# Layer 1's depthwise convolution spread over its projections and attention, branch products put between gate streams, two modulation sections moved into layer 0's attention

## The chip, the cores and the metric

One Trainium2 chip, one of its cores. The metric is the device time of one execution in microseconds (us). The kernel before took 1978.15 us (median of 3 runs, 1974.14 to 1978.68).

## What is computed

Two layers of a diffusion backbone over 512 latent tokens with 256 context tokens before them. Each layer has a token mixer with three branches (pooling, attention, convolution) under gates, then an MLP. Layer 1 is the last and computes latent outputs only; its context rows give keys and values alone. All arithmetic is float32.

```python
hl = _modulate(xl, sh1_l, sc1_l)                      # LayerNorm, then scale and shift from w_mod
ul_pool, ul_q, ul_k, ul_v, ul_conv, ul_gate = _split_in(hl @ w_in[i] + b_in[i])
ol = _latent_attention(ql, kl, vl, kc, vc, attn_sink[i])   # +-128 tokens, plus all context keys
y_conv = silu(layer_norm(depthwise_conv31(a * sigmoid(b)))) @ w_proj
yl = (g_pool * y_pool + g_attn * y_attn + g_conv * y_conv) @ w_out   # g = sigmoid(gates)
xl = _post_norm(xl, g1_l, yl, ln1_g[i], ln1_b[i])
xl = _post_norm(xl, g2_l, _mlp(_modulate(xl, sh2_l, sc2_l), ...), ln2_g[i], ln2_b[i])
```

`mod = silu(c) @ w_mod[i] + b_mod[i]` has six sections of 1024 (shift, scale, gate, for mixer and MLP); sections 3 and 4 are the MLP's shift and scale.

## The kernel before, in words

A float32 operand is kept as two fp32r halves (high and rest), so each product is three matmuls: high by high, rest by high, high by rest. Activations lie in `A` and `B` (tiles acta and actb, h and l; the names swap between layers), 8 slices of 128 channels by 768 columns. A weight unit is 128x512: one DMA into `raw`, a cast on ScalarE (`wh`, L134), a subtraction on GpSimd or VectorE (`wl`, L137). `weight_a` makes two units, one 128-column output tile for 8 contraction slices; `mm_a_steps` (L149) runs its 24 matmuls on 512 or 256 columns.

`w_phase` (L560) is the mixer of a layer. Its order: V and K projections, the queries of the first key-value head, the second pool tile; then the convolution (`conv`, L312): 31 chained VectorE instructions for each of two channel tiles; `cover` gives TensorE gate tiles meanwhile, for 145000 columns in layer 0 and 118000 in layer 1. Then pool products, LayerNorm of the convolution (`conv_norm`, a Sigmoid in it), and attention: 2 heads by 4 blocks (layer 0 has 4 more blocks for context). The queries of the second head are projected when its first block begins.

TensorE's order is written by hand: `tick` counts columns; `later` puts a step in a heap that falls due after so many columns, and between steps the generator `gated_steps` (L624) fills in. It runs 8 gate tiles for attention (to DRAM, `sgd`), then for each m a pool gate with its branch product (`branch_steps`, two contraction slices, 6 matmuls) and a conv gate with its product, and sends the sum to DRAM (`mfd`). A gate is a Tanh on ScalarE out of PSUM (L611); a product is combined with it on VectorE (L621). Gate and projection tiles take their PSUM banks from `psg` (two), branch products, the attention output and other small things from `psa` (two), scores and transposed probabilities from `pss` (two tiles of two banks). The other engines' instructions are ordered by a scheduler that keeps the program's priorities.

`pace` calls a generator once per so many columns. `mod_steps` (L173) makes one section: per contraction slice a chunk of `wmod`, and four matmuls of 32 weight columns by 256, one for each quarter of the PSUM partitions (float32, two TensorE records each). In layer 0, section 2 is paced over the projections; sections 3 and 4 over the closing stretch, which is the rest of the gates and then, for each m, the attention branch's product with `g` and `d` read back from DRAM (L827 to L835).

Of the kernel before, what the change touches and what calls it, by code (L numbers as in the profile page):

```python
# [18 lines left out]
P = 128  # L19
D = 1024  # L20
# [47 lines left out]
W_VAL = 9000  # L68
W_CONV0 = 145000
W_CONV1 = 118000  # L70
# [7 lines left out]
def backbone(ctx: ExitStack, tc: tile.TileContext, I: dict, out: bass.AP):  # L78
# [233 lines left out]
    def conv(pool, psum, cvec, gls, st):  # L312

        n = TL if st == 0 else TC
        ps = psum.tile([P, 1024], F32, tag="S", name=uid("cp"))
        accs = []
        for j in range(2):
            gl, run = gls[j, st], ps[:, j * 512:j * 512 + n]
            acc = pool.tile([P, n], F32, tag=f"ca{st}", name=uid("ca"), bufs=2)
            V.tensor_scalar(out=run, in0=gl[:, 0:n], scalar1=cvec[:, j, 0:1], scalar2=cvec[:, j, 31:32],  # L320
                            op0=ALU.mult, op1=ALU.add)
            for k in range(1, CK):
                V.scalar_tensor_tensor(out=run if k < CK - 1 else acc, in0=gl[:, k:k + n],
                                       scalar=cvec[:, j, k:k + 1], in1=run, op0=ALU.mult, op1=ALU.add)
            accs.append(acc)
        return accs

    def conv_norm(pool, scratch, cvec, accs, st, dst):
# [4 lines left out]
        for b0 in range(0, n, 256):  # L333
            pt, pb = bank(), bank()
# [12 lines left out]
            yield W_CN  # L347
            for j in range(2):
# [62 lines left out]
    def softmax_pv(pp, pss, g, Pt, vtiles, negm, sums, V_, sink, dst, qsl):  # L411
# [42 lines left out]
        t1 = pp.tile([64, 4, P], F32, tag="t1", name=uid("t1"), bufs=1)  # L454
        S.copy(t1, po[64:128, :].rearrange("p (a q) -> p a q", a=4))
        ot = pp.tile([P, 2, P], F32, tag="ot", name=uid("ot"), bufs=2)
# [6 lines left out]
    def attn_ctx(pp, pss, g, nb, Q, KH, KL, V_, nsink, sink, dst):  # L463
# [3 lines left out]
        for a in range(4):  # L467
            o = s[:, a * 256:(a + 1) * 256]
            T.matmul(o, Q[a][:, qsl], KH[g][:, CS], start=True, stop=False)
            T.matmul(o, Q[a][:, qsl], KL[g][:, CS], start=False, stop=True)  # L470
# [15 lines left out]
    def attn_lat(pp, pss, g, n, Q, KH, KL, V_, nsink, sink, dst, masks):  # L486
# [10 lines left out]
        for a in range(4):  # L497
            s = pss.tile([P, 1024], F32, tag="S", name=uid("S"))
            q = Q[a][:, qsl]
# [60 lines left out]
    def w_phase(i, A, B, has_ctx, pre, todo):  # L560
# [5 lines left out]
        with ExitStack() as ph:  # L566
# [8 lines left out]
            mg = ph.enter_context(tc.tile_pool(name=f"mg{i}", bufs=4 if todo else 6, reuse_waits="tile"))  # L575
            sgd = [dram.tile([P, W], F32, tag=f"sg{i}{m}", name=uid("sgd")) for m in range(KD)]
            mfd = [dram.tile([P, W], F32, tag=f"mf{i}{m}", name=uid("mfd")) for m in range(KD)]
            mix = ph.enter_context(ExitStack())
# [14 lines left out]
            if todo:  # L593
                pace((x for s in todo for x in mod_steps(i, s, 0, D, lambda: mg.tile(
                    [P, W], F32, tag="sg", name=uid("wm"))[:, :512])), 10000, 20000)
# [7 lines left out]
            def gate_steps(m, b):  # L603
# [10 lines left out]
            def branch_steps(w, ks, w0, g, outs, pool):  # L614

                while ks[0] not in mixed:
                    yield None
                for _, sl in outs:
                    ps = bank(pool)[:, :sl.stop - sl.start]
                    yield from mm_a_steps(w, B, ks, [(ps, sl)], w0)  # L620
                    V.scalar_tensor_tensor(out=g[:, sl], in0=g[:, sl], scalar=1.0, in1=ps,  # L621
                                           op0=ALU.add, op1=ALU.mult)

            def gated_steps():  # L624
                for m in range(KD):
                    g = yield from gate_steps(m, 1)
                    nc.sync.dma_start(out=sgd[m], in_=g)

                w, d, e, ahead = {}, {}, {}, 0 if todo else 2
                for m in range(ahead):  # L630
                    d[m] = yield from gate_steps(m, 0)
                for m in range(KD + 1):
                    if m + ahead < KD:
                        d[m + ahead] = yield from gate_steps(m + ahead, 0)
                    if m < KD:
                        w[m] = weight_a(I["wbr"][i, m][:, 0:4 * P])
                        yield from branch_steps(w[m], (0, 1), 0, d[m], outs_all, side["bank"])
                    if m:
                        e = yield from gate_steps(m - 1, 2)
                        yield from branch_steps(w.pop(m - 1), (2, 3), 2, e, outs_all, side["bank"])  # L640
                        G.tensor_tensor(out=d[m - 1], in0=d[m - 1], in1=e, op=ALU.add)
                        nc.sync.dma_start(out=mfd[m - 1], in_=d.pop(m - 1))

            mixed, side = set(), {"bank": psa}
# [11 lines left out]
            masks = kv.tile([P, 2, P], F32R, tag="masks", name=uid("masks"))  # L656
            KH = [kv.tile([P, TA], F32R, tag=f"kh{g}", name=uid("kh")) for g in range(NKV)]
            KL = [kv.tile([P, TA], F32R, tag=f"kl{g}", name=uid("kl")) for g in range(NKV)]
            V_ = kv.tile([P, 6, NKV, P], F32R, tag="V", name=uid("V"))

            def evac(ps, t):
                qf = kv.tile([P, TA], F32, tag="qf", name=uid("qf"))
                for st, p_ in enumerate(ps):
                    sl = (LS, CS)[st]
                    S.activation(qf[:, sl], p_, AF.Identity, bias=b_in[:, t:t + 1])
                return qf

            def query(Q, g, jj, temp):
                t = T_Q + 2 * g + jj
                qf = evac(proj(t, LC), t)  # L670
                rope(temp, qf, cs)
                for par in range(2):
# [16 lines left out]
            flush()  # L689

            vf = evac(proj(T_V, [LS, CS]), T_V)
# [14 lines left out]
            kf = evac(proj(T_K, [LS, CS]), T_K)  # L706
            rope(scratch("rt")[:, :TL], kf, cs)
            for g in range(NKV):
                r = slice(64 * g, 64 * g + 64)
                V.tensor_copy(KH[g][r, :], kf[r, :])  # L710
                S.copy(KH[g][64 - 64 * g:128 - 64 * g, :], kf[r, :])
                for r2 in (0, 64):
                    V.tensor_tensor(out=KL[g][r2:r2 + 64, :], in0=kf[r, :],
                                    in1=KH[g][r, :].bitcast(F32), op=ALU.subtract)
            Q = [kv.tile([P, W], F32R, tag=f"q{a}", name=uid("q")) for a in range(4)]
# [6 lines left out]
            def pool_products():  # L722
                for j in range(2):
# [6 lines left out]
                    for st, sl in outs_all:  # L730
                        n = TL if st == 0 else TC
                        ps = bank()[:, :n]
# [9 lines left out]
            accs = {st: conv(cp, pss, cvec, gls, st) for st, _ in outs_all}  # L742
            cover((W_CONV0 if has_ctx else W_CONV1) - W_PC)
            for wait in pool_products():
                cover(wait)
            mixed.add(0)
            cover(W_PC)
            flush()
            for st, _ in outs_all:
                for wait in conv_norm(cp, scratch, cvec, accs[st], st, B):  # L750
                    cover(wait)
            mixed.add(2)
            t12.close()
            pp = mix.enter_context(tc.tile_pool(name=f"pp{i}", bufs=1, side="right", reuse_waits="tile"))

            def items():
                for g in range(NKV):
                    if g:
                        Q[:] = [kv.tile([P, W], F32R, tag=f"q{a}", name=uid("q")) for a in range(4)]
                        for jj in range(2):  # L760
                            query(Q, g, jj, pp.tile([P, TL], F32, tag="rt", name=uid("rt"), bufs=1))
                    for n in range(4):
                        yield attn_lat(pp, pss, g, n, Q, KH, KL, V_, nsink, sink, B, masks)
# [49 lines left out]
            mixed.add(4)  # L813
            mix.close()
            if todo:
                for _ in pe["pace"]:
                    pass
            pace(None, 0)
# [3 lines left out]
            side["bank"] = psg  # L822
            if todo:
                pace((x for s in (3, 4) for x in mod_steps(i, s, 0, D, lambda: fin.tile(
                    [P, D], F32, tag="wm", name=uid("wm"), bufs=4))), 9000)
            drain(other)
            for m in range(KD):  # L827
# [4 lines left out]
                nc.sync.dma_start(out=d, in_=mfd[m])  # L832
# [3 lines left out]
            if todo:  # L836
                for _ in pe["pace"]:
# [231 lines left out]
    with tc.manual_schedule(engines={mybir.EngineType.PE}):  # L1069
# [69 lines left out]
        for i in range(DEPTH):  # L1139
            last = i == DEPTH - 1  # L1140
            w_phase(i, A, B, not last, pre, () if i else (2,))
# [87 lines left out]
```

## Time and profile before

| what | us |
|---|---|
| median of three runs | 1978.15 |
| the profiled execution, its own time | 1975.67 |
| its span, first to last instruction | 1973.9 |
| TensorE busy in the span | 1848.6 (94%) |
| VectorE / ScalarE / GpSimd busy | 1200.3 / 730.8 / 771.6 |
| mean granted TensorE clock, share of full | 0.978 |
| layer 0: attention | 244 to 476 |
| layer 0: closing stretch of the mixer | 476 to 543.2 |
| layer 1: projections and convolution | 1232 to 1353 |
| layer 1: attention | 1353 to 1528 |
| layer 1: closing stretch | 1528 to 1550.2 |

The times inside the span count from its first instruction. TensorE's records overlap: a matmul of 512 columns is shown with 0.39 us, and the next one begins 0.23 us later, so the work on this engine is counted by the distance between starts.

### The profile page before, as it was taken

The numbers are of one execution on the slowest core, as the hardware profiler recorded it, in microseconds if no ns is written. First come the engines' busy times: TensorE is split into PE (matmuls) and PEld (weight loads), VectorE is DVE, ScalarE is ACT, GpSimd is POOL, SyncE is SP. The second block draws the span as 40 slices with busy tenths as digits, with TensorE's granted clock in tenths as the row PEclk, the third lists the DMA queues.
The fourth block names the chain that finished last, engine by engine and source line by source line (L and its number), as shares of the span: only waits on it lengthen the run. The fifth ranks groups of instructions, "written<-read, shape, count | busy, mean of one in ns | idle before, by whom it ended". The sixth has DMA issues, their size and how long they took to land. (4 is left out here: it accounts for less than half of the span.)

```text
span 1973.9 us, 27007 instructions
## 1 busy us (share of the span) xinstructions
PE 1848.6 (94%) x9910; PEld 1548.4 (78%) x9910; DVE 1200.3 (61%) x2067; ACT 730.8 (37%) x1359; POOL 771.6 (39%) x629
## 2 busy tenths in 40 slices
PE   6999899899899999999999988999988989999997
PEld 4788788787678888888788868777866768888886
DVE  6489655654478946865533584786575784333356
ACT  4432255353234422233133344434444354333331
POOL 3653432322434422222122546664342554333343
PEclk8999999999999999999999989999999989999999
DMA  8523111114865434464422423141212753332341
GB/s 304 176 90 118 62 59 46 53 44 154 281 219 190 161 112 133 155 213 143 146 62 86 129 96 105 61 149 63 69 65 96 260 189 118 96 96 86 107 129 43
DMA packets 117557, 244.94 MB, mean 124 GB/s; under 512 B 14608, under 2 KB 16944, under 8 KB 117424
## 3 DMA queue, kind: packets, MB, share of 16 engines
q1 hardware_dynamic: 117424, 243.21, 38.0%
q8 instruction: 78, 1.28, 0.3%
q14 instruction: 55, 0.45, 0.1%
HBM read 223.20 MB, written 19.96 MB: 123 GB/s over the span
## 5 line engine op out<-in xcount | busy, mean ns | idle before, releaser
L137 POOL TENSOR_TENSOR wl<-raw,wh 128x512 fp32r<-128x512 f32 x371 | 516.7, 1405 | 783.6 <-ACT wh L134 698.9
L134 ACT CAST wh<-raw 128x512 fp32r<-128x512 f32 x506 | 310.8, 621 | 596.0 <-PE ps L167 292.1
L156 PE MATMUL ps<-actbh,wh 128*128 128x512 f32 (+1 forms) x1016 | 353.4, 348 | 14.3 <-DVE sg L621 6.9
L156 PE MATMUL ps<-actbl,wh 128*128 128x512 f32 (+1 forms) x1016 | 348.3, 343 | 3.1 <-POOL actbl L251 3.1
L156 PE MATMUL ps<-actbh,wl 128*128 128x512 f32 (+1 forms) x1016 | 347.8, 342 | 2.7 <-DVE rs L261 1.3
L156 PE MATMUL ps<-actah,wh 128*128 128x512 f32 (+1 forms) x928 | 331.4, 357 | 13.7 <-ACT actah L248 4.7
L156 PE MATMUL ps<-actal,wh 128*128 128x512 f32 (+1 forms) x928 | 327.4, 353 | 3.3 <-DVE actal L1097 1.9
L156 PE MATMUL ps<-actah,wl 128*128 128x512 f32 (+1 forms) x928 | 326.9, 352 | 0.4 <-POOL wl L137 0.3
L156 PEld LDWEIGHTS ps<-actbh,wh 128*128 128x128 f32 x1016 | 194.5, 191 | 45.2 <-DVE sg L621 10.0
L156 PEld LDWEIGHTS ps<-actbh,wl 128*128 128x128 f32 x1016 | 194.4, 191 | 25.6 <-DVE wl L137 2.4
L156 PEld LDWEIGHTS ps<-actbl,wh 128*128 128x128 f32 x1016 | 194.6, 192 | 23.3 <-POOL actbl L251 3.8
L156 PEld LDWEIGHTS ps<-actah,wh 128*128 128x128 f32 x928 | 177.5, 191 | 43.8 <-ACT actah L248 5.1
L156 PEld LDWEIGHTS ps<-actal,wh 128*128 128x128 f32 x928 | 177.6, 191 | 25.6 <-DVE actal L1097 2.2
L156 PEld LDWEIGHTS ps<-actah,wl 128*128 128x128 f32 x928 | 177.4, 191 | 24.2 <-POOL wl L137 1.0
L165 PE MATMUL ps<-wh,actah 128*128 128x512 f32 x480 | 192.6, 401 | 2.2 <-DVE acc L977 2.0
L167 PE MATMUL ps<-wh,actal 128*128 128x512 f32 x480 | 190.5, 397 | 3.5 <-DVE actal L251 3.5
L166 PE MATMUL ps<-wl,actah 128*128 128x512 f32 x480 | 190.1, 396 | 0.0
L137 DVE TENSOR_TENSOR wl<-raw,wh 128x512 fp32r<-128x512 f32 x135 | 127.8, 947 | 99.9 <-ACT wh L134 97.3
L204 DVE SCALAR_TENSOR_TENSOR wm<-wm,sc,wm 128x512 f32<-128x512 f32 x140 | 124.4, 924 | 67.1 <-DMA wm<-in_wmod 67.0
L970 DVE TENSOR_TENSOR acc<-ps,acc 128x512 f32<-128x512 f32 x140 | 94.7, 684 | 95.3 <-PE ps L167 95.2
L165 PE MATMUL ps<-wh,actbh 128*128 128x512 f32 (+1 forms) x328 | 127.2, 388 | 1.5 <-DVE fg L621 1.5
L166 PE MATMUL ps<-wl,actbh 128*128 128x512 f32 (+1 forms) x328 | 126.8, 387 | 1.0 <-POOL wl L137 1.0
(207 smaller groups left out, 2721.7 us busy)
## 6 DMA issues: line engine op xcount, KB each, us to landing
raw<-in_w SPq DMA_DIRECT2D x264, 256.0 KB
raw<-in_win SPq DMA_DIRECT2D x154, 256.0 KB
wm<-in_wmod SPq DMA_DIRECT2D x72, 512.0 KB
raw<-in_wout SPq DMA_DIRECT2D x56, 256.0 KB
wm<-in_wmod SPq DMA_DIRECT2D x48, 256.0 KB
raw<-in_wbr SPq DMA_DIRECT2D x32, 256.0 KB
x1d<-R SPq DMA_DIRECT2D x10, 512.0 KB
acc<-in_b SPq DMA_DIRECT2D x10, 512.0 KB
```

The source lines that it names most:

```text
L134: S.copy(wh, r)
L137: e.tensor_tensor(out=wl, in0=r, in1=wh[:].bitcast(F32), op=ALU.subtract)
L156: T.matmul(ps, w(hl, w0 + n), x[xi][:, k, sl], start=(start and first and hl == 0 and xi == 0), stop=(stop and last and hl == 1))
L165: T.matmul(ps, x[0][:, k0 + k, tsl], wh, start=(k == 0), stop=False)
L166: T.matmul(ps, x[0][:, k0 + k, tsl], wl, start=False, stop=False)
L167: T.matmul(ps, x[1][:, k0 + k, tsl], wh, start=False, stop=(k == n - 1))
L204: V.scalar_tensor_tensor(out=o, in0=x, scalar=sc[:, k, r:r + 1], in1=o, op0=ALU.mult, op1=ALU.add)
L970: V.tensor_add(a, ps, a)
```

## The change

1. Sections 3 and 4 of layer 0's modulation go from the closing stretch into attention, one step per 3500 columns; their chunks are 256 columns wide (three buffers), and `mod_steps` yields after each of the four matmuls where the chunk holds only one of them.
2. A branch product is no longer run behind its gate: `gate_steps` queues it in `pend` as one `piece` per stream, and a piece runs between the streams of the next gate, with its PSUM bank from `psg`.
3. In layer 1 the convolution is paced, one VectorE instruction per 2400 columns, from the V projection on, in two `psa` banks; pool products and `conv_norm` become steps that fall due; attention begins after 35000 columns of gates. The second head's queries are projected inside the first head's blocks. Pool parts go to DRAM and are read back when the conv part is there. V and the masks lie in free columns of `B`.
4. In both layers the high halves of K and Q are copied on ScalarE; the second copy of K's rest is a ScalarE copy too.

```diff
@@ mod_steps
                 T.matmul(ps[32 * j:32 * j + 32, :q], sc[:, k, :], w[:, o:o + q],
                          start=(k == 0), stop=(k == KD - 1))
+                if w.shape[-1] == q and j < 3:
+                    yield
             yield
@@ conv -> conv_steps
+    def conv_steps(pool, banks, cvec, gls, st, accs):
...
-            gl, run = gls[j, st], ps[:, j * 512:j * 512 + n]
+            gl, run = gls[j, st], banks(j)[:, :n]
...
                 V.scalar_tensor_tensor(out=run if k < CK - 1 else acc, in0=gl[:, k:k + n],
                                        scalar=cvec[:, j, k:k + 1], in1=run, op0=ALU.mult, op1=ALU.add)
+                yield
@@ gate_steps
                     S.activation(g[:, sl], ps, AF.Tanh, bias=bg[:, t:t + 1], scale=0.5)
+                    if pend:
+                        yield from pend.pop(0)
+                if w2:
+                    pend.extend(piece(w2, ks, ks[0], g, o, done if o is outs_all[-1] else None)
+                                for o in outs_all)
                 return g
+            def piece(w, ks, w0, g, o, done):
                 while ks[0] not in mixed:
                     yield None
+                yield from branch_steps(w, ks, w0, g, [o], psg)
+                if done:
+                    done(g)
@@ gated_steps, layer 1
+                if not has_ctx:
+                    for m in range(KD):
+                        w = weight_half(m)
+                        yield from gate_steps(m, 0, w, (0, 1), lambda g, m=m: nc.sync.dma_start(
+                            out=mfd[m], in_=g))
+
+                    def merge(m, e):
+                        d = mg.tile([P, W], F32, tag="sg", name=uid("sg"))
+                        nc.sync.dma_start(out=d, in_=mfd[m])
+                        G.tensor_tensor(out=d, in0=d, in1=e, op=ALU.add)
+                        nc.sync.dma_start(out=mf2[m], in_=d)
+
+                    for m in range(KD):
+                        w = weight_half(m)
+                        yield from gate_steps(m, 2, w, (2, 3), lambda e, m=m: merge(m, e))
...
@@ query
-                    V.tensor_copy(q[r, :W], qf[r, :W])
-                    V.tensor_tensor(out=q[ro, :W], in0=qf[r, :W], in1=q[r, :W].bitcast(F32),
-                                    op=ALU.subtract)
+                    S.copy(q[r], qf[r])
+                    V.tensor_tensor(out=q[ro], in0=qf[r], in1=q[r].bitcast(F32), op=ALU.subtract)
@@ layer 1
+            def convolution():
+                accs = []
+                yield from conv_steps(cp, lambda j: bank(), cvec, gls, 0, accs)
+                later(W_CT, stages(conv_norm(cp, scratch, cvec, accs, 0, B), 2))
+
+            if not has_ctx:
+                pace(convolution(), EV_CONV)
...
+                cover(W_QR)
+                later(W_PU, stages(pool_products(), 0))
...
+            if todo:
+                for _ in pe["pace"]:
+                    pass
+                pace((x for s in todo[1:] for x in mod_steps(i, s, 0, D, lambda: pp.tile(
+                    [P, 256], F32, tag="wm", name=uid("wm"), bufs=3))), EV_MOD)
...
+                        if not has_ctx and g == 0 and n in (1, 2):
+                            nq = nq or [B[0][:, 2 * a:2 * a + 2, CS] for a in range(4)]
+                            query(nq, 1, n - 1, rope_temp())
@@ closing stretch
-            if todo:
-                pace((x for s in (3, 4) for x in mod_steps(i, s, 0, D, lambda: fin.tile(
-                    [P, D], F32, tag="wm", name=uid("wm"), bufs=4))), 9000)
             drain(other)
```

How the orders move at three places:

TensorE in layer 0. `wm` is a chunk of `w_mod`, `sc` the condition vector. Before, in the closing stretch, the four matmuls of a slice stand together (x4) between matmuls of a branch product:

```order
L156 MATMUL ps_4882<-actbh,wh_4352 128x256
L156 MATMUL ps_4882<-actbl,wh_4352 128x256
L156 MATMUL ps_4882<-actbh,wl_4353 128x256
L185 MATMUL ps_4886<-wm_4887,sc 32x256 x4
L156 MATMUL ps_4882<-actbh,wh_4352 128x256
```

Now, in attention (`S` scores, `pth` and `ptl` the transposed probabilities, `V` the values):

```order
L517 MATMUL S_2791<-kh_783,q_1212 128x256
L518 MATMUL S_2791<-kl_785,q_1212 128x256
L189 MATMUL ps_2566<-wm_2802,sc 32x256
L160 MATMUL ps_2787<-actbh,wh_2172 128x256
L160 MATMUL ps_2787<-actbl,wh_2172 128x256
L160 MATMUL ps_2787<-actbh,wl_2173 128x256
L160 MATMUL ps_2824<-actah,wh_2813 128x512
L160 MATMUL ps_2824<-actal,wh_2813 128x512
L160 MATMUL ps_2824<-actah,wl_2814 128x512
L458 MATMUL ps_2762<-pth_2772,V_782 128x512
L459 MATMUL ps_2762<-ptl_2773,V_782 128x512
```

Where 16 groups of four stood, 64 single matmuls now stand, each between matmuls of the whole array.

VectorE in layer 1 before, from the last query (`q`) to the convolution (`cp`, then `ca`) and the first pool product's result (`py`):

```order
L677 TENSOR_TENSOR q_11815<-qf_11964,q_11815 64x512
L323 SCALAR_TENSOR_TENSOR cp_11974<-gl_11602,cvec_11557,cp_11974 128x512
L250 CAST pwh_12429<-pw_12427 128x128
L323 SCALAR_TENSOR_TENSOR cp_11974<-gl_11602,cvec_11557,cp_11974 128x512 x13
L323 SCALAR_TENSOR_TENSOR ca_11975<-gl_11602,cvec_11557,cp_11974 128x512
L320 TENSOR_SCALAR cp_11974<-gl_11609,cvec_11557 128x512
L323 SCALAR_TENSOR_TENSOR cp_11974<-gl_11609,cvec_11557,cp_11974 128x512 x29
L323 SCALAR_TENSOR_TENSOR ca_12007<-gl_11609,cvec_11557,cp_11974 128x512
L250 CAST actah<-py_12443 128x512
```

Now, at the first maxima of the scores (`mx`, `ngm`):

```order
L329 SCALAR_TENSOR_TENSOR ca_11774<-gl_11706,cvec_11653,ps_11773 128x512
L329 SCALAR_TENSOR_TENSOR ps_12184<-gl_11713,cvec_11653,ps_12184 128x512
L520 TENSOR_REDUCE mx_12238<-S_12240 128x1
L329 SCALAR_TENSOR_TENSOR ps_12184<-gl_11713,cvec_11653,ps_12184 128x512
L521 SCALAR_TENSOR_TENSOR ngm_12237<-mx_12238,nsink_11667 128x1
L329 SCALAR_TENSOR_TENSOR ps_12184<-gl_11713,cvec_11653,ps_12184 128x512 x2
L520 TENSOR_REDUCE mx_12238<-S_12277 128x1
```

Of the convolution's 62 instructions 48 now stand ahead of the first maximum and 14 among the first block's, the two channel tiles in turn; before, all 62 stood ahead of attention.

ScalarE in layer 1's attention now (`cs` the Sigmoid of `conv_norm`, `P` the exponentials); before, the four Sigmoids stood ahead of the one table load:

```order
L365 ACTIVATE cs_12873<-cy_12871 128x256
L463 COPY pth_12919<-ps_12673 64x512
L138 CAST wh_13195<-raw_13193 128x512
L625 ACTIVATE sg_12833<-ps_12834,bg_11669 128x512
L524 ACT_TABLE_LOAD
L524 ACTIVATE P_12937,sums_12928<-S_12929,ngm_12926 128x512
L452 CAST pth_12952<-pt_12943 128x512
L452 CAST pth_12956<-pt_12943 128x512
L365 ACT_TABLE_LOAD
L365 ACTIVATE cs_13002<-cy_13000 128x256
L524 ACT_TABLE_LOAD
L524 ACTIVATE P_12993,sums_12928<-S_12985,ngm_12926 128x512
```

The whole program had 4 table loads and now has 10.

## Rows read from the trace of the kernel before

**Rows 1.** Windows: stretch, PE, PEld, DVE, ACT, POOL busy (records), clock, DMA share, GB/s.

```profile
244.00:476.00 232.00, 219.87 (x1320) 190.96 (x1318) 133.91 (x271) 112.18 (x245) 68.26 (x54) 0.99 0.16 51
476.00:543.20 67.20, 57.66 (x390) 42.32 (x391) 27.45 (x39) 17.04 (x26) 30.07 (x19) 0.97 0.86 296
1232.00:1287.00 55.00, 52.32 (x245) 43.30 (x246) 40.75 (x64) 21.71 (x42) 37.58 (x29) 0.97 0.18 58
```

**Rows 2.** Timeline of PE around one group of the modulation: start, length, instruction.

```profile
483.53 0.39 PE L156 MATMUL ps<-actah,wl 128*128 128x512 f32 x1
483.85 0.64 PE L185 MATMUL ps<-wm,sc 128*32 128x256 f32 x8
...
484.75 0.39 PE L156 MATMUL ps<-actal,wh 128*128 128x512 f32 x1
```

**Rows 3.** Timeline of PE at the end of layer 0's closing stretch.

```profile
532.86 1.50 PE L185 MATMUL ps<-wm,sc 128*32 128x256 f32 x24
...
543.24 0.78 PE L165 MATMUL ps<-wh,actah 128*128 128x512 f32 x1
...
546.38 0.42 PE L166 MATMUL ps<-wl,actah 128*128 128x512 f32 x1
```

**Rows 4.** Waits of PE, 244 to 476: us in total, times, longest.

```profile
PE ps L156 <- DVE sg L621: 4.0, 6, 1.4
PE S L501 <- ACT P L515: 3.4, 1, 3.4
PE ps L156 <- ACT qf L665: 2.6, 3, 1.0
```

**Rows 5.** Timeline at a gate of 256 columns, its last matmul and its Tanh.

```profile
178.75 0.28 PE L156 MATMUL ps<-actah,wl 128*128 128x256 f32 x1
...
179.52 0.47 ACT L611 ACTIVATE sg<-ps,bg 128x256 f32<-128x256 f32 x1
```

**Rows 6.** Waits of PE, layer 1, 1232 to 1550.2.

```profile
PE S L501 <- DVE q L677: 5.5, 1, 5.5
PE ps L351 <- DVE cn L345: 3.4, 2, 2.8
PE ps L452 <- DVE ptl L446: 2.7, 7, 0.8
PE ps L736 <- POOL pwl L251: 2.1, 1, 2.1
PE ps L451 <- ACT pth L445: 2.1, 3, 0.7
```

**Rows 7.** Windows, columns as in rows 1.

```profile
1450.00:1460.00 10.00, 10.00 (x43) 8.50 (x44) 4.46 (x11) 4.75 (x11) 2.77 (x2) 0.78 0.11 33
```

**Rows 8.** Timeline of DVE in layer 1's projections.

```profile
1238.86 0.81 DVE L320 TENSOR_SCALAR cp<-gl,cvec 128x512 f32<-128x512 f32 x1
...
1249.67 0.42 DVE L702 TENSOR_TENSOR V<-vt,V 128x256 fp32r<-128x256 f32 x1 [9.21 <-ACT V L701]
...
1286.19 0.74 DVE L323 SCALAR_TENSOR_TENSOR cp<-gl,cvec,cp 128x512 f32<-128x512 f32 x1
1286.85 1.12 DVE L409 TENSOR_TENSOR qf<-qf,rt 128x512 f32<-128x512 f32 x1
...
1292.09 3.92 DVE L323 SCALAR_TENSOR_TENSOR cp<-gl,cvec,cp 128x512 f32<-128x512 f32 x5
```

**Rows 9.** Groups of DVE by line and form, 1230 to 1360: count, busy us, mean ns.

```profile
L713 DVE TENSOR_TENSOR kl<-qf,kh 64x768 fp32r<-64x768 f32 x4 | 5.8, 1453 | 0.1
L676 DVE CAST q<-qf 64x512 fp32r<-64x512 f32 x4 | 3.3, 828 | 0.1
...
L710 DVE CAST kh<-qf 64x768 fp32r<-64x768 f32 x2 | 1.5, 772 | 0.0
```

**Rows 10.** Timeline of ACT at layer 1's first exponential.

```profile
1355.33 1.28 ACT L515 ACT_TABLE_LOAD   x1 [1.71 <-DVE ngm L512]
1356.63 0.69 ACT L515 ACTIVATE P<-S,ngm 128x512 f32<-128x512 f32 x1
```

More of the change, by code (lines that the diff above doesn't have):

```diff
@@ L593, in w_phase @@
             if todo:
-                pace((x for s in todo for x in mod_steps(i, s, 0, D, lambda: mg.tile(
+                pace((x for s in todo[:1] for x in mod_steps(i, s, 0, D, lambda: mg.tile(
                     [P, W], F32, tag="sg", name=uid("wm"))[:, :512])), 10000, 20000)
@@ L627, in gated_steps @@
                     nc.sync.dma_start(out=sgd[m], in_=g)
-                w, d, e, ahead = {}, {}, {}, 0 if todo else 2
-                for m in range(ahead):
-                    d[m] = yield from gate_steps(m, 0)
+                if not has_ctx:
[11 more added lines that the diff above has]
+                        yield from gate_steps(m, 2, w, (2, 3), lambda e, m=m: merge(m, e))
+                    while pend:
+                        yield from pend.pop(0)
+                    return
@@ L632, in gated_steps, with merge @@
+                w, d = {}, {}
+                def merge(m, e):
+                    G.tensor_tensor(out=d[m], in0=d[m], in1=e, op=ALU.add)
+                    nc.sync.dma_start(out=mfd[m], in_=d.pop(m))
                 for m in range(KD + 1):
-                    if m + ahead < KD:
-                        d[m + ahead] = yield from gate_steps(m + ahead, 0)
                     if m < KD:
-                        w[m] = weight_a(I["wbr"][i, m][:, 0:4 * P])
-                        yield from branch_steps(w[m], (0, 1), 0, d[m], outs_all, side["bank"])
+                        w[m] = weight_half(m)
+                        d[m] = yield from gate_steps(m, 0, w[m], (0, 1))
@@ L638, in gated_steps @@
                     if m:
[L639 to L644, printed above, removed]
+                        yield from gate_steps(m - 1, 2, w.pop(m - 1), (2, 3), lambda e, m=m: merge(m - 1, e))
@@ L689, in w_phase, with stages @@
             flush()
-            vf = evac(proj(T_V, [LS, CS]), T_V)
+            def stages(gen, branch):
+                yield 0
+                wait = next(gen, None)
+                if wait is None:
+                    mixed.add(branch)
+                else:
+                    later(wait, stages(gen, branch))
+            def convolution():
[4 more added lines that the diff above has]
+                pace(convolution(), EV_CONV)
+            vf = channels(T_V, [LS, CS])
             def values():
@@ L709, in w_phase, with queries @@
                 r = slice(64 * g, 64 * g + 64)
[L710 to L715, printed above, removed]
+                r2 = slice(64 - 64 * g, 128 - 64 * g)
+                S.copy(KH[g][r, :], kf[r, :])
+                S.copy(KH[g][r2, :], kf[r, :])
+                V.tensor_tensor(out=KL[g][r, :], in0=kf[r, :], in1=KH[g][r, :].bitcast(F32), op=ALU.subtract)
+                S.copy(KL[g][r2, :], KL[g][r, :].bitcast(F32))
+            def queries():
+                return [kv.tile([P, W], F32R, tag=f"q{a}", name=uid("q"))[:, :].rearrange(
+                    "p (b c) -> p b c", c=TC) for a in range(4)]
+            Q = queries()
             query(Q, 0, 0, scratch("rt")[:, :TL])
@@ L754, in w_phase @@
-            pp = mix.enter_context(tc.tile_pool(name=f"pp{i}", bufs=1, side="right", reuse_waits="tile"))
+            if has_ctx:
+                accs = {}
+                for st, _ in outs_all:
+                    big = pss.tile([P, 1024], F32, tag="S", name=uid("cp"))
+                    accs[st] = []
+                    for _ in conv_steps(cp, lambda j: big[:, 512 * j:512 * j + 512], cvec, gls, st, accs[st]):
+                        pass
+                cover(W_CONV0 - W_PC)
+                for wait in pool_products():
+                    cover(wait)
+                mixed.add(0)
+                cover(W_PC)
+                flush()
+                for st, _ in outs_all:
+                    for wait in conv_norm(cp, scratch, cvec, accs[st], st, B):
+                        cover(wait)
+                mixed.add(2)
+                t12.close()
+            else:
+                cover(W_QR)
+                later(W_PU, stages(pool_products(), 0))
@@ L756, in items @@
             def items():
+                nq = None
                 for g in range(NKV):
                     if g:
-                        Q[:] = [kv.tile([P, W], F32R, tag=f"q{a}", name=uid("q")) for a in range(4)]
-                        for jj in range(2):
-                            query(Q, g, jj, pp.tile([P, TL], F32, tag="rt", name=uid("rt"), bufs=1))
+                        Q[:] = nq or queries()
+                        if not nq:
+                            for jj in range(2):
+                                query(Q, g, jj, rope_temp())
@@ L836, in w_phase @@
             if todo:
-                for _ in pe["pace"]:
+                for _ in pe["pace"] or ():
                     pass
```

95 lines of the change are left out of this document (54 added, 41 removed).

## The prediction, on record before the changed kernel ran

> **What bounds the kernel now.** I read the views in this order: windows by stage, the TensorE (PE) timeline, PE's waits by stage, then the timelines of VectorE (DVE) and ScalarE (ACT) where they end those waits.
>
> The windows [rows 1] say that PE is the bound: 219.87 us busy of 232 in layer 0's attention, 57.66 of 67.2 in its closing stretch, 52.32 of 55 in layer 1's projections. A matmul of 512 columns starts 0.227 us after the one before, of 256 columns 0.12. So a change can win only idle time (12.1 us in that attention, 9.5 in that closing stretch), time at half clock, and work taken from PE. The second window differs from the others: its DMA share is 0.86 at 296 GB/s, against 0.16 at 51 in attention. Chunks of `wmod` fill the DMA engines there.
>
> In the timeline the reader is to see what a group of four modulation matmuls costs [rows 2]: from 483.53 to 484.75 stand two ordinary matmuls and one group, 1.22 us; less 2 x 0.227 a group costs 0.77. At the stretch's end [rows 3] three groups in a row last 1.50, one alone 0.64 [rows 2]; each further group thus costs 0.43. I read that as 0.43 for the columns (256, two passes, the four quarters at once) and 0.34 for going from the whole array to a quarter and back. After it, from 543.24 to 546.38, seven starts stand 0.43 apart or a little more: half of full speed, after a stretch in which PE mostly waited.
>
> PE's waits in layer 0's attention [rows 4]: 4.0 us for a `psa` bank that VectorE's combination frees, 3.4 for probabilities, 2.6 for query evictions. A gate's eviction is in [rows 5]: the last matmul starts at 178.75, its Tanh ends at 179.99, 1.24 later. In layer 1 [rows 6] PE waits for the second head's queries (5.5), the convolution's norm (3.4), rests and halves of the probabilities (2.7, 2.1), a pool weight (2.1), and a stretch of attention after the gates are used up has the clock at 0.78 [rows 7]. VectorE's timeline there [rows 8] begins the convolution at 1238.86, sits idle 9.21 us behind a V step, and makes a step each 0.66 us (1286.19 to 1286.85) beside other work or 0.78 (3.92 for 5) in a chain. The groups [rows 9] price the casts and subtractions for K and Q; [rows 10] shows the table load ahead of an exponential, 1.28 us.
>
> **The change part by part.** Layer 0.
>
> *Sections 3 and 4 out of the closing stretch.* Sixteen groups: ten within the stream, 10 x 0.77 = 7.7 [rows 2], and the tail of six from 532.86 to 543.24, 10.4 us, mostly waits for chunks [rows 3]. The half clock behind it, 7 x (0.45 - 0.227) = 1.6. Of the 9.5 idle us about 1.7 lie ahead of the tail. Sum -21.4 (bounds -18, if the half clock and other waits stay, and -24).
>
> *The same sections in attention.* 64 single matmuls instead of 16 groups. No row shows a single one: 0.19 if it costs a quarter of a group, 0.77 if a whole one [rows 2]. A single one streams the same 256 columns twice and changes the array's shape twice, so I take 0.72, near the upper bound: 64 x 0.72 = +46 (12 to 49). The rows show four in one group beginning together, their price being the columns' and the switch's.
> The Trainium skill, "TensorEngine Tiling (Array Packing)", section Tiling Modes, Key Properties, says that a change of the tiling mode drains TensorE; that speaks against this change, which has four times as many switches. By the rule alone 64 switches at 0.34 would be 22 where 16 were 5; the trace agrees as far as a group costs more than its columns.
> Their chunks add 8.4 MB over 232 us, 36 GB/s on 51 [rows 1]: free by share. A chunk has three buffers, so SP may hold weight loads behind it (a rival).
>
> *Waits in attention.* The pieces leave `psa` for `psg`: the 4.0 go; the singles give cover where PE waited 3.4 + 2.6 [rows 4]. -10 (bounds 0 and -12.1, all idle).
>
> *A wait added.* A piece now uses the gates' two banks: gate half, piece, gate half. Behind a 256-column half stands a piece of 6 x 0.12 = 0.72, and the next but one use needs the Tanh's end at 1.24 [rows 5]: about 0.4 short, 16 times, 6.4 at most; behind a 512 half (6 x 0.227 = 1.36, more with its eviction) it fits. Where an attention step stands between, nothing is lost: +3 (0 to 12, the second bound for VectorE freeing a piece's bank late).
>
> Layer 0: -21.4 + 46 - 10 + 3 = +17.6.
>
> Layer 1. *Won*: gates stand beside all of the first attention blocks, and queries are projected a block ahead: 5.5 + 3.4 + 2.7 + 2.1 + 2.1 [rows 6], and ten us at 0.78 [rows 7] give back 2.2. -18 (0 to -24).
>
> *First scores.* By my count of the new order PE passes V, K, two queries, one pool tile (32.7 us) and 35000 columns of gates (15.5) from 1238.9 on, and is at the first score by 1287; a third score needs a buffer back, by 1292.3. VectorE must do 48 convolution steps before its first maximum, at 0.70 between the two spacings [rows 8]: 33.6. From 1238.86 to 1292.09 it took 53.2, of which 9.2 idle and sixteen convolution steps 11.8, so other work 32; less the casts and second rests that go to ScalarE, 3.3 + 1.5 + half of 5.8 = 7.7 [rows 9]: 24.4. First maximum at about 1297, then the small step 0.3, a table load and an exponential (1.28 + 0.69 [rows 10]): 1299. PE waits some 7, and 1.5 more behind it: +8 (0 to 16).
>
> *Tables.* Four loads become ten; six x 1.28 = 7.7 on ScalarE, in the blocks with Sigmoids, of which PE sees under half: +3 (0 to 8). In [rows 10] the exponential starts 0.02 after the load.
> The Trainium skill, "ScalarE: Activation LUTs", What ACT_TABLE_LOAD costs, has some 2.66 us per switch, a drain included; six would be 16. The row here shows no drain behind the load; ahead of it the engine was idle, so a drain could hide.
>
> *VectorE's queue.* Fourteen convolution steps lie among the first blocks' maxima: +2 (0 to 8).
> The store and reload of pool parts (4 MB, 16 transfers) and GpSimd's addition lie 8 gates ahead of their use: nothing, hidden by attention; without that cover some 2 us each.
>
> Layer 1: -18 + 8 + 3 + 2 = -5.
>
> **Sum**: +12.6 on the profiled execution's 1975.67, 1988.3; the median of the runs is 2.5 above that execution, so 1990 on its footing.
>
> **Rivals.** (A) *The cover holds.* The point is VectorE's pace: if the convolution with its other work is through by 1292 rather than 1297, and the tables fall in cover, layer 1 gives -18 or more, -24 with the smaller waits; layer 0 loses all its 12.1 idle and no gate waits: -21.4 + 46 - 12.1 = +12.5. Between -5 and -11: about 1970. For it: ScalarE has 21.71 busy of 55 [rows 1], so it can take the casts. Against: VectorE, 40.75 of 55, gains little room. Faster.
> (B) *Half of that.* Layer 0 at +12.5, layer 1 at -12 as the score wait stays and the rest is covered: about 0, 1979. No change.
> (C) *A single costs a quarter*, if what a group spends is one column of tiles after another: 46 becomes 12, the sum -21: 1957. Against it: three groups in 1.50 [rows 3], with the four starting together.
> (D) *SP holds weights back.* A chunk's transfer waits for its buffer, one step being 3500 columns or 1.55 us; loads of `raw` stand behind it in SP's queue. Decisive from the point where a unit lands less than that ahead of its cast; at every fourth of 64 steps 16 x 1.55 = 25 more: about 2014.
>
> **How the numbers follow.** Forecast (1983 to 2002, slower) 0.40; A 0.22; B 0.20; C 0.08; D 0.10. About 0.3% (6 us) is what a measurement of this kernel can tell from no change. Faster 0.22 + 0.08 = 0.30, same 0.20, slower 0.50. The range takes the forecast's band with B, most of A down to 1960 and D's nearer half up to 2012: it leaves out C and the ends, under 2 in 10. The likeliest case's own range is 1983 to 2002.
>
> **What would show it.** Right: in layer 0's attention single modulation matmuls with the next matmul some 0.7 us behind; that attention 30 to 40 us longer, the closing stretch some 20 shorter, its DMA share far below 0.86; no PE wait for VectorE's combination there. In layer 1 a wait of 5 to 10 us at the third score, ten table loads, no 5.5 for queries. Wrong: singles at 0.2 to 0.4 (C); a third score without wait (A); PE waits for ScalarE's cast of `raw`, with DMA behind it, all through attention (D); or gates waiting for Tanh by far more than 3 us.

## The result, and the profile after

The changed kernel took 1999.99 us (median of 4 runs, 1994.38 to 2006.65), the kernel before 1976.14 beside it (4 runs, 1971.34 to 1978.68): ratio 1.0125, 95% interval 1.0084 to 1.0166. It is slower, by 24 us. The forecast was 1990, slower, with a range of 1960 to 2012. The profiled execution is the run of 2006.65, span 2004.7; the stages of both profiles, from one matmul of TensorE to another:

| stage | before | after | difference | forecast |
|---|---|---|---|---|
| to layer 0's first score | 244.6 | 248.7 | +4.1 | 0 |
| layer 0, attention | 231.4 | 267.3 | +35.9 | +39 |
| layer 0, closing stretch | 67.2 | 48.0 | -19.2 | -21.4 |
| layer 0, MLP and modulation | 650.6 | 657.6 | +7.0 | 0 |
| layer 1, mixer | 356.4 | 359.3 | +2.9 | -5 |
| layer 1, MLP | 412.9 | 412.9 | 0 | 0 |

The fourth row is not the change's: its code is the same, and in the fourteen profiles of this study that stage lasts 647.3 to 660.3, without order by kernel. The other rows add up to 23.7; the measured difference is 23.9. The rows come from one profile each: the same code of layer 1's mixer took 359.3, 361.6 and 360.3 us in three profiles (the changed kernel, e1, e3), so a difference of 3 us in such a row says nothing.

The windows (as in [rows 1]) of layer 0's attention and closing stretch now:

```profile
248.70:516.00 267.30, 261.42 (x1439) 197.96 (x1437) 131.08 (x267) 114.55 (x245) 67.97 (x55) 1.00 0.24 76
516.00:564.00 48.00, 47.69 (x274) 41.77 (x273) 23.14 (x36) 14.79 (x23) 27.82 (x17) 1.00 0.76 259
```

TensorE's idle time fell from 12.1 to 5.9 us in the one and from 9.5 to 0.3 in the other: the covers worked. But busy time in the two rose by 32 us, with the same matmuls. TensorE's timeline in attention shows on what:

```profile
300.56 0.39 PE L160 MATMUL ps<-actal,wh 128*128 128x512 f32 x1
300.79 0.40 PE L160 MATMUL ps<-actah,wl 128*128 128x512 f32 x1
301.12 0.62 PE L189 MATMUL ps<-wm,sc 128*32 128x256 f32 x2
301.67 0.50 PE L160 MATMUL ps<-actah,wh 128*128 128x512 f32 x1
302.00 0.40 PE L160 MATMUL ps<-actal,wh 128*128 128x512 f32 x1
```

From 300.79 to 302.00 stand two matmuls of 512 columns and one single modulation matmul (two records): 1.21 less 2 x 0.227 is 0.76. A group of four cost 0.77 [rows 2]. The example is typical: taken in the same way, 62 of the 64 singles cost 0.74 to 0.81 us, with a median of 0.75. So at 0.76 the 64 singles cost 48.6 us where 16 groups cost 12.3. The trace also shows why: a single's two records begin at 301.12 and 301.36, 0.24 apart; in the group of [rows 2] four begin between 483.85 and 483.87 and the other four between 484.09 and 484.11. The four quarters run at the same time, and one quarter alone takes as long.

TensorE's waits in layer 0's attention, to compare with [rows 4]:

```profile
PE ps L160 <- ACT qf L719: 2.0, 3, 1.0
PE ps L189 <- DMA wm<-in_wmod: 1.7, 1, 1.7
PE ps L160 <- DVE sg L645: 0.9, 2, 0.5
PE ps L160 <- ACT sg L625: 0.8, 2, 0.6
```

The wait of 4.0 for VectorE's combination is 0.9, the 3.4 for probabilities is gone, and gates wait 0.8 for a Tanh, not 3. Chunks cost one wait of 1.7, and there is none for a cast of `raw`, so nothing shows that SP held weights back.

Ahead of attention stands a wait that no step of the prediction had. ScalarE's timeline in layer 0:

```profile
149.18 1.68 ACT L731 CAST q<-qf 64x768 fp32r<-64x768 f32 x2 [11.09 <-DVE qf L416]
150.89 0.69 ACT L625 ACTIVATE sg<-ps,bg 128x512 f32<-128x512 f32 x1
```

and TensorE's at the same place, then in layer 1:

```profile
145.24 0.28 PE L160 MATMUL ps<-actah,wl 128*128 128x256 f32 x1
151.63 0.79 PE L160 MATMUL ps<-actah,wh 128*128 128x512 f32 x1 [6.11 <-ACT sg L625]
...
1314.50 0.80 PE L160 MATMUL ps<-actbh,wh 128*128 128x512 f32 x1 [5.61 <-ACT sg L625]
```

The copy of Q's high half, moved to ScalarE by the change's fourth part, waits for the rope on VectorE. ScalarE stands idle ahead of it for 11.09 us, a finished gate's Tanh stands behind it, and TensorE waits for that gate's bank. The windows behind the two waits show the granted clock at 0.50, the lower of its two levels (1.2 GHz):

```profile
151.60:155.00 3.40, 3.37 (x8) 2.69 (x9) 3.37 (x7) 1.38 (x3) 2.53 (x2) 0.50 0.15 36
1314.50:1318.00 3.50, 3.50 (x8) 2.82 (x9) 3.47 (x6) 2.08 (x4) 3.16 (x4) 0.50 0.50 172
```

Behind the first wait 13 matmuls of 512 columns start 0.43 us apart instead of 0.227, up to 157.34; behind the second eight do, up to 1318.08. That costs 2.8 and 1.8 us on top of the waits.

TensorE's waits in layer 1's mixer, to compare with [rows 6]:

```profile
PE S L510 <- ACT P L524: 10.4, 8, 2.7
PE ps L160 <- ACT sg L625: 5.6, 1, 5.6
PE ps L344 <- DVE cy L362: 3.2, 1, 3.2
...
PE ps L459 <- DVE ptl L453: 0.2, 1, 0.2
```

The 5.5 for queries and the waits for halves and rests of the probabilities went. In their place stand 10.4 for scores' buffers and 5.6 for the gate. Only 0.9 of the 10.4 is at the third score; the rest, 9.5 in seven waits, lies in later blocks, from 1345 to 1510. The longest of these waits of TensorE ends at an exponential that stands behind two table loads on ScalarE:

```profile
1410.64 0.58 PE L510 MATMUL S<-kh,q 128*128 128x256 f32 x1 [2.73 <-ACT P L524]
```

```profile
1406.79 1.28 ACT L365 ACT_TABLE_LOAD   x1
1408.08 0.42 ACT L365 ACTIVATE cs<-cy 128x256 f32<-128x256 f32 x1
1408.51 1.28 ACT L524 ACT_TABLE_LOAD   x1
1409.81 0.69 ACT L524 ACTIVATE P<-S,ngm 128x512 f32<-128x512 f32 x1
```

VectorE in this layer, with convolution steps (L329) on both sides of the first maximum (L520):

```profile
1323.84 0.75 DVE L329 SCALAR_TENSOR_TENSOR ps<-gl,cvec,ps 128x512 f32<-128x512 f32 x1
1324.49 0.68 DVE L520 TENSOR_REDUCE mx<-S 128x1 f32<-128x512 f32 x1
1325.10 0.74 DVE L329 SCALAR_TENSOR_TENSOR ps<-gl,cvec,ps 128x512 f32<-128x512 f32 x1
```

### The profile page after: what moved, and what is told of

It is laid out like the page before. It is cut to its first block, busy times and chain, and to the rows that moved or that the text cites. A ratio compares the mean times of both kernels' runs of the same rounds, so it can differ in the third digit from the quotient of the medians.

```text
span 2004.7 us, 27174 instructions
## 1 busy us (share of the span) xinstructions
PE 1883.6 (94%) x9910; PEld 1558.1 (78%) x9910; DVE 1182.5 (59%) x2051; ACT 761.1 (38%) x1397; POOL 769.0 (38%) x629
## 3 DMA queue, kind: packets, MB, share of 16 engines
q8 instruction: 78, 1.28, 0.3%
## 5 line engine op out<-in xcount | busy, mean ns | idle before, releaser
L160 PE MATMUL ps<-actah,wh 128*128 128x512 f32 (+1 forms) x928 | 337.5, 364 | 18.1 <-ACT sg L625 6.9
L141 DVE TENSOR_TENSOR wl<-raw,wh 128x512 fp32r<-128x512 f32 x143 | 134.9, 944 | 119.0 <-ACT wh L138 118.6
L171 PE MATMUL ps<-wh,actbl 128*128 128x512 f32 (+1 forms) x328 | 127.4, 388 | 0.0
```

Source lines behind the costliest of these rows:

```text
L141: e.tensor_tensor(out=wl, in0=r, in1=wh[:].bitcast(F32), op=ALU.subtract)
L160: T.matmul(ps, w(hl, w0 + n), x[xi][:, k, sl], start=(start and first and hl == 0 and xi == 0), stop=(stop and last and hl == 1))
L171: T.matmul(ps, x[1][:, k0 + k, tsl], wh, start=False, stop=(k == n - 1))
```

## Experiments

My theory after these readings: the loss is the singles, 48.6 us against 12.3; ScalarE's copy adds some ten; layer 1's part is worth nothing because VectorE is late. The rival: singles fall into cover, and the loss is in ScalarE and layer 1.

**Groups of four in attention (e1).** The changed kernel, with the edit below; the rope's temporary also takes a buffer of the probabilities, to make room for the fourth chunk.

```diff
-EV_MOD = 3500
+EV_MOD = 14000
...
-                if w.shape[-1] == q and j < 3:
-                    yield
...
-                    [P, 256], F32, tag="wm", name=uid("wm"), bufs=3))), EV_MOD)
+                    [P, 256], F32, tag="wm", name=uid("wm"), bufs=4))), EV_MOD)
```

> The changed kernel, its 64 single modulation matmuls in layer 0's attention put back into 16 groups of four, each every 14000 columns (a fourth chunk buffer, for which the rope's temporary takes a buffer of the probabilities). Theory (a single costs as much as a group, 0.76 us in the profile of the changed kernel): 48 x 0.76 = 36 us less than the changed kernel, 1964 us, ratio to before 0.994. Rival (a single costs little, the loss is in ScalarE's copies and layer 1): no more than 12 us less, ratio 1.006 or above.

1965.93 us, ratio 0.9944 (0.9924 to 0.9964): the theory's 0.994. Its timeline:

```profile
294.21 0.39 PE L160 MATMUL ps<-actah,wl 128*128 128x512 f32 x1
294.53 0.64 PE L189 MATMUL ps<-wm,sc 128*32 128x256 f32 x8
295.10 0.50 PE L160 MATMUL ps<-actah,wh 128*128 128x512 f32 x1
295.44 0.39 PE L160 MATMUL ps<-actal,wh 128*128 128x512 f32 x1
```

Four matmuls take 1.23 less 0.454, 0.77 us: what a single one takes. With the singles put back into groups the changed kernel is faster than the kernel before.

**Q's copies on VectorE again (e2).**

```diff
-                    S.copy(q[r], qf[r])
+                    V.tensor_copy(q[r], qf[r])
```

> The changed kernel, with the high halves of Q copied on VectorE again. Theory (ScalarE, in order, stands 11.1 and 9.5 us on the first such copy, a Tanh behind it, and PE waits 6.1 and 5.6 us for that gate's bank): 8 to 11 us less than the changed kernel, ratio to before 1.007. Rival (VectorE then is later at the first maximum by eight copies of 0.83 us, and the waits come back as waits for scores or queries): between 3 us less and 4 us more, ratio 1.011 to 1.014.

1993.6 us, ratio 1.0085 (1.0068 to 1.0102). That is some 8 us below the changed kernel's 1.0125, but the two intervals overlap, so the times alone don't settle it; the stages do. Up to layer 0's first score it takes 237.0 us, not 248.7, and the wait for the gate is gone. Over all profiles that stage is 247.1 to 248.8 in the three with ScalarE's copies there and 237.0 to 241.0 in the eight with VectorE's, so 11.7 is the largest such difference and some 9 the usual one. In layer 1 the rival held: the mixer is 364.6, not 359.3, since the wait came back at the third score, the longest in these waits of TensorE:

```profile
PE S L510 <- ACT P L524: 17.8, 6, 9.9
```

**Sections 3 and 4 back in the closing stretch (e3).** The call of `pace` as in the kernel before, all else as changed.

> The changed kernel, with sections 3 and 4 back in layer 0's closing stretch as groups of four; all else as changed. Theory (singles are the loss): +21.4 for the closing stretch, -48.6 for the 64 singles, +6 for waits in attention that they covered: 21 us less than the changed kernel, ratio to before 1.001. Rival (the rest of the change is the loss): as the changed kernel or slower, ratio 1.012 or above.

1975.41 us, ratio 0.9983 (0.9963 to 1.0002). A little below the theory's 1.001, far from the rival's 1.012: without the move the rest of the change is worth some 3 us, at most 7, and by the interval perhaps nothing. From layer 0's first score to its MLP it takes 294.6 us, the kernel before 298.7. The pieces on gates' banks may have won these 4, but no run takes them apart from the rest. Its start has ScalarE's copy too (248.8 to the first score).

**The kernel before, with singles in attention (e4), and with groups (e6).** Only the two sections moved (with them, the `side` bank is `psg` in layer 0, and the rope's temporary and the output go into other tiles' buffers).

```diff
+            if todo:
+                for _ in pe["pace"]:
+                    pass
+                pace((x for s in (3, 4) for x in mod_steps(i, s, 0, D, lambda: pp.tile(
+                    [P, 256], F32, tag="wm", name=uid("wm"), bufs=3))), EV_MOD)
...
-            if todo:
-                pace((x for s in (3, 4) for x in mod_steps(i, s, 0, D, lambda: fin.tile(
-                    [P, D], F32, tag="wm", name=uid("wm"), bufs=4))), 9000)
```

> The kernel before with one part of the change: sections 3 and 4 in layer 0's attention as 64 single matmuls (its branch products there with banks of the gates' pool, because the section holds one of the others; smaller temporaries). Theory (0.76 us each): +48.6 - 21.4 - 10 = +17 us, ratio 1.009. Rival (a single costs a quarter, the loss is elsewhere): -21 + 12 - 10 = -19 us, ratio 0.990.

> The kernel before with sections 3 and 4 in layer 0's attention as 16 groups of four, as in the experiment before-with-singles but for the groups. Theory: 48 x 0.76 = 36 us less than with singles, 1964 us, ratio 0.993; the rest of the change then is worth nothing against it. Rival (the singles of that kernel fell partly into idle time that groups can't fill): 25 us less, ratio 0.999.

With singles 2000.03 us, ratio 1.0115 (1.0095 to 1.0136): this part alone gives nearly the whole loss. With groups 1971.29, 0.9968 (0.9949 to 0.9988). The two differ by 0.0147, 29 us, between the 36 and the 25 expected. Some singles did fall into waits that groups leave open: in attention TensorE waits 2.6 for probabilities with groups, 1.4 with singles, and 2.4 against 0.8 for VectorE's combination. That is 2.8 of the 7 us; the rest is no more than the intervals allow.

**Layer 1: more gates ahead of attention (e5, e7, e8).** All from the kernel of groups, with `W_QR` 60000; in e5 and e8 all of Q's copies on VectorE, in e7 those of layer 0, and in e8 also a Tanh in place of the convolution's Sigmoid.

```diff
-W_QR = 35000
+W_QR = 60000
```

> The kernel of the groups of four (e1), with the high halves of Q copied on VectorE in both layers, and layer 1's attention begun after 60000 columns of gates instead of 35000. In the VectorE-copy experiment layer 0's mixer came out some 11 us shorter and layer 1's some 5 longer, with PE waiting 9.9 us at the third score. Theory (that wait is VectorE late with the convolution, and 25000 columns, 11 us, of gates ahead of the first score cover it): 11 + 4 = 15 us less than e1, ratio to before 0.987. Rival (the wait only moves to a later block, or gates are then missing behind attention): 7 us less at most, ratio 0.991 or above.

> As e5, but VectorE copies in layer 0 alone; ScalarE copies stay in layer 1. Theory (in layer 1 either copy costs a wait, ScalarE's a gate's bank 5.6 us, VectorE's a later score; with 60000 columns VectorE's is covered and ScalarE's is not): 3 to 5 us more than e5, ratio 0.989. Rival (with VectorE relieved layer 1 is shorter): 3 us less than e5, ratio 0.9855.

> As e5, and the Sigmoid of the convolution's norm written with Tanh (x/2 times 1 + tanh(x/2)), so that the program has 4 table loads again and not 10. Theory (under half of six x 1.28 us reached PE): 3 us less than e5, ratio 0.9855. Rival (the loads lie in cover): no difference from e5 within 1 us. A rule by which a switch costs 2.66 us would give up to 8 us.

Copies on VectorE in both layers: 1963.69 us, ratio 0.9919 (0.9894 to 0.9944). My theory fell here: 25000 columns did not cover the wait. Copies on ScalarE in layer 1: 1956.91, 0.9884 (0.9854 to 0.9915), where I had put it behind. VectorE in the first, then TensorE's wait at the third score:

```profile
1287.66 11.04 DVE L327 SCALAR_TENSOR_TENSOR ps<-gl,cvec,ps 128x512 f32<-128x512 f32 x14
1298.61 0.68 DVE L518 TENSOR_REDUCE mx<-S 128x1 f32<-128x512 f32 x1
```

```profile
1300.88 0.58 PE L508 MATMUL S<-kh,q 128*128 128x256 f32 x1 [9.84 <-ACT P L522]
```

The later start let the scheduler set 61 of the 62 convolution steps ahead of the first maximum; in the changed kernel 48 are. The wait moved along with VectorE's queue. The rival's number held; its place, a later block, did not, for the wait is at the third score again.

The Tanh in place of the Sigmoid: 1963.62, 0.9923 (0.9896 to 0.9949), no difference from e5. The profile of e5 has 8 table loads and not the 10 of the changed kernel, since its Sigmoids fall elsewhere; e8 has 4. So four loads fewer, 5.1 us of ScalarE, made no difference there. For the changed kernel, where two waits end behind loads, this was not run. The Trainium skill, "ScalarE: Activation LUTs", What ACT_TABLE_LOAD costs, has 2.66 us per switch, a drain included; by it the four would be 10.6 us of ScalarE, an estimate. The trace does not agree: in the changed kernel the load at 1408.51 begins 0.01 us after a Sigmoid's end and the exponential 0.02 after the load, so a switch takes 1.31 us.

**Both waits at once (e9 to e12).** In `query`, VectorE copies in layer 0 and, in layer 1, for the one query on which ScalarE stood; beside it, and then together with it, 90000 columns.

```diff
+                    (V.tensor_copy if has_ctx or (g == 0 and jj == 1) else S.copy)(q[r], qf[r])
```

> As e7 (VectorE's copies in layer 0, ScalarE's in layer 1, groups of four, 60000 columns of gates), but in layer 1 the second query of the first head is copied on VectorE too: the copy on which ScalarE stood while a gate's Tanh waited 5.6 us. Theory (that wait is the copy's place in ScalarE's order): 5.6 us won, 2 us of VectorE time lost at the first maximum: 3.5 us less than e7, ratio 0.9866. Rival (what e5 lost is any copy on VectorE there, its queue being the limit): no gain or up to 5 us more, ratio 0.9885 to 0.991.

> As e7, with 90000 columns of gates ahead of layer 1's attention. Theory (VectorE reaches the first maximum at its own time, whatever stands on TensorE; 30000 columns, 13 us, more cover what e7 still waits for scores, 3.6 us): 2 to 4 us less than e7, ratio 0.987. Rival (more convolution steps and pool work move ahead of the maximum, or gates are missing at the end of attention): no gain or up to 5 us more, ratio 0.9885 to 0.991.

One copy on VectorE with 60000 columns: 1964.48 us, ratio 0.9924 (0.9901 to 0.9947); the gate's wait is gone, and the score's is 11.1. ScalarE's copies with 90000: 1955.88, 0.9883 (0.9844 to 0.9922), no better than with 60000; its waits:

```profile
PE ps L160 <- ACT sg L623: 6.6, 2, 5.6
PE S L508 <- ACT P L522: 4.5, 5, 1.4
```

Both rivals held, e9 even beyond its rival's band. But the profiles fit one reading. Counted from the last product of layer 0's MLP, in us (first score on TensorE, first maximum on VectorE, longest wait for a score, wait for the gate, whole mixer of layer 1):

| kernel | columns | first score | first maximum | score | gate | mixer |
|---|---|---|---|---|---|---|
| as changed | 35000 | 100.1 | 102.9 | 2.7 | 5.6 | 359.3 |
| all copies VectorE (e2) | 35000 | 95.9 | 107.6 | 9.9 | - | 364.6 |
| all copies VectorE (e5) | 60000 | 108.0 | 121.0 | 9.8 | - | 359.7 |
| ScalarE's in layer 1 (e7) | 60000 | 114.7 | 116.4 | 1.3 | 5.6 | 350.2 |
| one on VectorE (e9) | 60000 | 104.1 | 117.6 | 11.1 | - | 355.7 |
| ScalarE's in layer 1 (e10) | 90000 | 127.5 | 128.3 | 1.4 | 5.6 | 351.7 |

At 60000 columns VectorE comes to the first maximum at 116 to 121, whatever TensorE does, and between the first convolution step and that maximum it sits idle 2.5 to 3.9 us. VectorE is the bound of that stretch; a wait taken from TensorE in it comes back at its end (e9 against e7). In the changed kernel the two meet early because 14 convolution steps are left over, and its score waits lie in the blocks behind. The kernels with 60000 or more columns have 61 or 62 steps ahead of the first maximum and 8 table loads, so they gain in those blocks too; which of the two does it was not taken apart. TensorE must have other work until about 117, and no wait on the way. That gave the last two kernels.

> As e9 (one query's copy on VectorE in layer 1), with 90000 columns of gates ahead of layer 1's attention as in e10. From the start of layer 1's stretch TensorE had its first score at 104 us in e9 and VectorE its first maximum at 117.6; in e10 VectorE's last convolution step was at 115.6 and TensorE's score at 127.5, with the gate's wait of 5.6 still there. Theory (VectorE is the bound of that stretch, and a wait goes only if TensorE has other work until about 117 us): 30000 columns bring TensorE's first score from 104 to 117, neither wait is left, layer 1's mixer stretch is about 346 us (e9 355.7, e10 351.7), ratio 0.9855. Rival (VectorE gets more work ahead of the first maximum, or gates are missing later): a wait of 5 us or more at the third score, ratio 0.988 or above.

> As e5 (all of Q's copies on VectorE in both layers), with 90000 columns of gates ahead of layer 1's attention. In e5 TensorE's first score came at 108 us, VectorE's first maximum at 121. Theory: 30000 columns, 13 us, bring them together at 121; the 9.8 us at the third score go, layer 1's mixer stretch is about 349 us, ratio 0.987. Rival (a wait in the same place): 355 us or more, ratio 0.990 or above.

One copy on VectorE, 90000 columns: 1947.51 us, ratio 0.9861 (0.9832 to 0.989), mixer 346.5 where the theory had 346, first score at 120.1 where it had 117. All copies on VectorE: 1951.64, 0.9881 (0.985 to 0.9913), between its theory and its rival; mixer 351.1. In both the long waits are gone, with 1.4 the longest for a score and 1.1 for a gate. In the first of them VectorE now waits for TensorE, and not the other way about:

```profile
1297.70 0.69 DVE L518 TENSOR_REDUCE mx<-S 128x1 f32<-128x512 f32 x1 [0.28 <-PE S L516]
```

It has the lowest ratio of the study, 30 us under the kernel before and 52 under the changed one, though its interval overlaps those of e7, e10 and e12.

## Why the prediction was right, and where its size was off

*The single matmul at 0.72* was right: 0.76, shown by the timeline, and by two pairs of kernels that differ in this and in a chunk buffer (36 and 29 us). The rival that a single costs a quarter (C) fell. The Trainium skill ("TensorEngine Tiling (Array Packing)", Tiling Modes, Key Properties) has it that a change of the tiling mode drains TensorE. That points the right way; the trace adds that the columns count in full as well.

*The closing stretch* lost 19.2. Of the forecast's 21.4, 1.6 was the half clock behind it, so 19.2 stands against 19.8. That clock did rise (0.96 from 543.2 to 620 before, 1.00 from 564 to 642 now), but the first stretch of the MLP behind it is not shorter for it (75.9 us before, 78.1 now). The stretch's DMA share is 0.76, not "far below 0.86". *Attention* gained 35.9 where -10, +46 and +3 make 39; the gates' wait for Tanh was 0.8 and not 3, so the hold by the two banks hardly exists.

*What was put at nothing*: the casts "that go to ScalarE" were booked as VectorE's gain alone. Nowhere did the prediction ask what is queued behind such a copy in ScalarE's order. In layer 0's start it was a Tanh, and TensorE waited 6.1 us and then lost 2.8 at the lower clock, 8.9 together; the profiles with and without the copy differ by some 9. The whole stage is only 4.1 longer than before because it has other gains, which were not taken apart.

*Layer 1* has -5 in the forecast and came out no shorter (359.3 against 356.4). The first scores were sized right and put in the wrong place. From the first convolution step VectorE needed 57.3 us to the first maximum (forecast 33.6 + 24.4 = 58). TensorE needed 54.6 to the first score (forecast 32.7 + 15.5 = 48.2), of which the gate's wait and the clock behind it are 7.4. So the wait of 7 came at the gate and the third score waited 0.9: 8.3 in all for a forecast of 8. By the prediction's own list a third score without wait was A's sign; here it was not. With the copies back on VectorE the wait stood where forecast, 9.9 long, and the mixer was 5.3 longer. Two other terms were off. Of the 18 to be won, the queries' wait and those for halves and rests of the probabilities went, 10.3; waits for the convolution's norm (3.2 for 3.4) and for pool weights (1.9 for 2.1) stayed, and the mixer's mean clock fell from 0.98 to 0.96 instead of rising. And the later blocks wait 9.5 for scores, where +3 for *tables* and +2 for *VectorE's queue* were booked. Two of these waits, 1.7 and 2.7, end behind table loads, so the 3 may have been there; the shares were not measured apart.

*The sum* of +12.6 (1990.8 on the runs' footing, written as 1990) is about half of the measured 23.9. The direction and the range held because the two large terms, the singles and the closing stretch, were right; that layer 1's error and layer 0's start left the time inside the likeliest case's 1983 to 2002 is luck.

*Rival A* (layer 1 and the idle time won in full) named the right point, VectorE's time at the first maximum, and fell on it: 57.3 us after the first step is 1296 in its terms, not 1292. With 90000 columns and one copy moved, layer 1's mixer is 10 us shorter than before, of A's 18. *Rival D* fell: one chunk wait of 1.7 us in attention.

Not settled: why layer 0's MLP stage differs by 13 us between profiles, and what each of the smaller waits in layer 1 (3.2 for the convolution's norm) would give.

## What to carry to other kernels

Small matmuls that fill a quarter of TensorE's columns belong together: here one of them between matmuls of the whole array cost what four cost (0.76 and 0.77 us), so spreading them finer paid four times. Before moving a copy to an emptier engine, look at what it waits for and who stands behind it in that engine's order, however low its busy share. Where two engines wait for one another in turn, find which one is never idle: giving the other one more work until then is what removed the waits here; each removed alone only moved.

## What I had not expected of the hardware

A modulation matmul on a quarter of the columns cost as much alone as four on the four quarters (0.75 and 0.77 us, medians of 64 and 16). A wait of TensorE cost more than its length: behind 6.1 and 5.6 us the granted clock was 0.50 and 13 and 8 matmuls ran at half speed, 2.8 and 1.8 us more. And a table load between two busy activations took its 1.28 us and 0.03 around it, with no drain to be seen in the records.
